# Gate and up projections of four feed-forward blocks as seven block products, in three parts of columns

## The chip, the cores and the metric

One core of a Trainium2 chip runs the whole program once. The metric is the device time of that execution in microseconds (us). The matrix engine is called PE (its weight loads are shown apart, as PEld), the vector engine DVE, the scalar engine ACT, GpSimd POOL, and SP is the queue that issues the weight transfers. PSUM holds eight banks of [128, 512] float32; each bank is where PE writes. SBUF is the on-chip memory that the other operands lie in.

## The reference

Two transformer-like layers on 512 tokens of width 1024, all in float32. There are four feed-forward blocks, two in each layer, all of one shape: the input is normalized, multiplied by a [1024, 5632] matrix, split into a gate and an up half of 2816 columns, and `silu(gate) * up` is multiplied by a [2816, 1024] matrix.

```
def _rmsnorm(x, g):
    y = xf * lax.rsqrt(jnp.mean(xf * xf, axis=-1, keepdims=True) + EPS)
    return (y * g.astype(jnp.float32)).astype(x.dtype)

def _swiglu(x, w_in, w_out):
    gate, up = jnp.split(x @ w_in, 2, axis=-1)
    return (jax.nn.silu(gate) * up) @ w_out

# first layer
x = x + 0.5 * _swiglu(_rmsnorm(x, n1_g[l]), ffn1_w_in[l], ffn1_w_out[l])
...  # two attention mixers, gated and added
x = x + 0.5 * _swiglu(_rmsnorm(x, n3_g[l]), ffn2_w_in[l], ffn2_w_out[l])
return _rmsnorm(x, nf_g)
...  # second layer: feed-forward, stick-breaking attention, feed-forward
```

## The kernel before, in words

The residual stream is kept transposed: eight tiles `x[k]` of [128 features, 512 tokens]. A matrix product in float32 is made of three products of float32r pairs: an operand is split into a high part (a copy with rounding, on ACT) and a low part (operand minus high part, on DVE), and `mm3` (lines 178 to 181) adds high*high, high*low and low*high in a bank. Every matmul has a [128, 128] piece of weights, loaded for it, and 512 tokens that move.

`plan` lists all weights in the order of their use, in chunks of up to [128, 1024]. `load_ahead` issues their transfers on SP, `split_ahead` splits them into `wh` (ACT, L156) and `wl` (DVE, L157), four chunks ahead of their use, and `weight` hands them out.

`ffn` (line 265) takes the 22 column blocks one after the other: a block is 128 gate columns and 128 up columns, 8 pieces of 128 features each, 48 matmuls. The gate is scaled by the tokens' norm `rs` (L274, DVE), goes through silu (L275, ACT), is multiplied with the up bank (L276, DVE) and split (L174 on ACT, L175 on DVE) into `hid`. The output projection then takes each of the eight output tiles with all 22 pieces of `hid` (66 matmuls), scales (L295) and adds to `x[m]` (L296), and `done(m)` starts what follows from `x[m]`. The norm's scale comes from squares (`Norm.add`: ACT squares, DVE adds), one matmul with ones (`total`, L232) and `rsqrt` (two ACT steps, three DVE steps). It is applied after the products, so PE needn't wait for it; the first `ffn` asks for it after its second column block (`at=1`).

PE, ACT and SP work in the order in which the program is written. On DVE and POOL a scheduler sets the order when the program is built. Each engine takes its instructions strictly in that order.

## Time and profile before

| what | value |
|---|---|
| runs | 2180.39, 2181.23, 2183.92 us (median 2181.23) |
| span of the profiled execution | 2182.6 us, 1.4 above the median |
| PE busy | 2153.3 us, 99% of the span, 9782 matmuls |
| PE weight loads busy | 1765.2 us, 81% |
| DVE busy | 1123.7 us, 51% |
| ACT busy | 883.0 us, 40% |
| POOL busy | 64.6 us, 3% |

A matmul's busy time runs from its start to its modelled end, and the next one starts before that end. So a busy PE is read by the distance from start to start and not by the sum of durations. DVE and ACT overlap their instructions a little in the same way. A row of the timeline or of the groups has the program's line, what was written and read, and the shape; `<-` at the end names who ended the idle time before it.

### The profile page before, as it was taken

Reading aid. Unit: us, or ns where it says so; the run is one execution under the profiler, and the core shown is the slowest. Engines: PE = TensorE matmul, PEld = TensorE weight load, DVE = VectorE, ACT = ScalarE, POOL = GpSimd, SP = SyncE. Lnnn points to the kernel's source line nnn. Section 1 sums busy time; section 2 is a strip of 40 time slices with the busy share of each in tenths; the row PEclk is TensorE's granted clock in tenths of the full one; section 3 lists DMA queues with packets and bytes.
Section 4 is the critical chain, followed back from the end, with each engine's and each line's share of the span. In section 5 each row is a group of like instructions: output and inputs, shape, how many; then the busy total and the mean of one; then the engine's idle time right before and its main releaser. Section 6 shows DMA issues by size and latency. Waiting matters only on the chain.

```text
span 2182.6 us, 24716 instructions
## 1 busy us (share of the span) xinstructions
PE 2153.3 (99%) x9782; PEld 1765.2 (81%) x9782; DVE 1123.7 (51%) x1659; ACT 883.0 (40%) x1415; POOL 64.6 (3%) x167
## 2 busy tenths in 40 slices
PE   8999999999999999999999999999999989999999
PEld 6888888887888788888888888888777768888887
DVE  6444334799843744444446444344687756444332
ACT  5222222376766442223233222223577665222211
POOL 0000000000000100000000000000011110000000
PEclk9999999999999999999999999999999999999999
DMA  4322233222211332222332222333111103222331
GB/s 163 111 97 98 82 105 119 89 87 73 70 48 49 117 104 97 97 96 81 105 104 91 99 98 94 92 96 97 58 44 44 49 19 107 97 97 97 97 120 53
DMA packets 57268, 193.42 MB, mean 89 GB/s; under 512 B 6784, under 2 KB 6784, under 8 KB 57152
## 3 DMA queue, kind: packets, MB, share of 16 engines
q1 hardware_dynamic: 55296, 188.28, 26.3%
q0 software_dynamic: 640, 2.10, 0.3%
q10 hardware_dynamic: 1216, 1.47, 0.2%
q8 instruction: 76, 1.25, 0.2%
q14 instruction: 40, 0.33, 0.0%
HBM read 189.07 MB, written 2.10 MB: 88 GB/s over the span
## 4 chain that ended last, share of the span: by engine, by line
PE 84%; issue 10%; DVE 4%; ACT 2%; DMA 0%; POOL 0%; SPq 0%; DVEq 0%; POOLq 0%
PE ps L179 25%; PE ps L180 25%; PE ps L181 25%; PE ps L803 2%; PE ps L869 1%; PE ps L848 1%; PE ps L732 1%; PE ps L734 1%; PE ps L733 1%; DVE wl L157 1%; PE ps L761 1%; PE ps L844 1%; PE ps L416 0%; PE ps L415 0%; DVE sl L498 0%
## 5 line engine op out<-in xcount | busy, mean ns | idle before, releaser
L179 PE MATMUL ps<-sl,wh 128*128 128x512 f32 x2704 | 1070.4, 396 | 11.5 <-ACT sl L246 6.6
L180 PE MATMUL ps<-sl,wh 128*128 128x512 f32 x2704 | 1055.7, 390 | 1.8 <-DVE sl L175 1.0
L181 PE MATMUL ps<-sl,wl 128*128 128x512 f32 x2704 | 1056.0, 391 | 0.0
L179 PEld LDWEIGHTS ps<-sl,wh 128*128 128x128 f32 x2704 | 509.7, 188 | 121.4 <-issue 7.0
L180 PEld LDWEIGHTS ps<-sl,wh 128*128 128x128 f32 x2704 | 509.6, 188 | 109.3 <-issue 3.4
L181 PEld LDWEIGHTS ps<-sl,wl 128*128 128x128 f32 x2704 | 509.1, 188 | 107.1 <-DVE wl L157 0.4
L157 DVE TENSOR_TENSOR wl<-wraw,wh 128x1024 fp32r<-128x1024 f32 (+3 forms) x368 | 434.8, 1183 | 289.5 <-ACT wh L156 289.0
L156 ACT ACTIVATE wh<-wraw 128x1024 fp32r<-128x1024 f32 (+3 forms) x368 | 372.9, 1015 | 520.6 <-issue 237.9
L174 ACT ACTIVATE sl<-sl 128x512 fp32r<-128x512 f32 x113 | 71.4, 632 | 394.9 <-DVE sl L276 384.0
L276 DVE TENSOR_TENSOR sl<-ps,sl 128x512 f32<-128x512 f32 x88 | 60.9, 692 | 267.2 <-PE ps L181 260.8
L274 DVE TENSOR_TENSOR sl<-ps,sl 128x512 f32<-128x512 f32 x88 | 60.8, 691 | 138.7 <-PE ps L181 138.6
L175 DVE TENSOR_TENSOR sl<-sl 128x512 fp32r<-128x512 f32 x113 | 79.9, 707 | 79.1 <-ACT sl L174 78.6
L227 ACT ACTIVATE sl<-x 128x512 f32<-128x512 f32 x42 | 25.8, 629 | 124.4 <-DVE x L296 97.7
L295 DVE SCALAR_TENSOR_TENSOR sl<-ps,sl 128x512 f32<-128x512 f32 x32 | 22.1, 691 | 80.0 <-PE ps L181 80.0
L275 ACT ACTIVATE sl<-sl 128x512 f32<-128x512 f32 x88 | 54.2, 616 | 12.2 <-DVE sl L274 12.2
L517 ACT ACTIVATE sl<-sl,mx 128x128 f32<-128x128 f32 (+3 forms) x64 | 35.9, 560 | 47.2 <-DVE mx L516 45.9
L823 POOL TENSOR_SCALAR_AFFINE_SELECT sl<-sl 128x128 f32<-128x128 f32 x64 | 23.1, 373 | 941.7 <-ACT sl L814 832.9
L594 PE MATMUL ps<-sl 128*128 128x256 f32 (+2 forms) x176 | 43.3, 327 | 1.3 <-DVE mx L516 1.3
L228 DVE TENSOR_TENSOR sl<-sl 128x512 f32<-128x512 f32 x49 | 33.3, 691 | 20.9 <-ACT sl L227 20.4
L524 ACT ACTIVATE sl<-sl,sm 128x128 f32<-128x128 f32 (+3 forms) x64 | 35.8, 559 | 15.8 <-DVE sm L523 7.3
L869 PE MATMUL ps<-sl 128*128 128x512 f32 (+3 forms) x128 | 38.7, 446 | 3.0 <-POOL sl L859 3.0
L817 DVE SCALAR_TENSOR_TENSOR sl<-ps,sl 128x512 f32<-128x512 f32 (+1 forms) x48 | 28.7, 597 | 24.2 <-ACT sl L815 23.8
(124 smaller groups left out, 1448.3 us busy)
## 6 DMA issues: line engine op xcount, KB each, us to landing
wraw<-in_f_in_dram SPq DMA_DIRECT2D x176, 512.0 KB
wraw<-in_f_out_dram SPq DMA_DIRECT2D x64, 512.0 KB
wraw<-in_mix_t_dram SPq DMA_DIRECT2D x34, 512.0 KB
wraw<-in_f_out_dram SPq DMA_DIRECT2D x32, 384.0 KB
wraw<-in_sb_qk_dram SPq DMA_DIRECT2D x16, 512.0 KB
wraw<-in_br_dram SPq DMA_DIRECT2D x16, 256.0 KB
wraw<-in_w_out_dram SPq DMA_DIRECT2D x8, 512.0 KB
wraw<-in_sb_v_dram SPq DMA_DIRECT2D x8, 512.0 KB
```

Source lines behind the costliest of these rows:

```text
L156: act.activation(wh[:, :n], raw[:, :n], AF.Copy)
L157: dve.tensor_tensor(wl[:, :n], raw[:, :n], wh[:, :n].bitcast(F32), op=OP.subtract)
L174: act.activation(h, x, AF.Copy)
L175: dve.tensor_tensor(l, x, h.bitcast(F32), op=OP.subtract)
L179: pe.matmul(ps, wh, xh, start=start, stop=False)
L180: pe.matmul(ps, wh, xl, start=False, stop=False)
L181: pe.matmul(ps, wl, xh, start=False, stop=stop)
L274: dve.tensor_tensor(g, pg, rs, op=OP.mult)
L275: act.activation(g, g, AF.Silu)
L276: dve.tensor_tensor(g, pu, g, op=OP.mult)
L803: pe.matmul(pz[b][:, c:c + w], k[hr, sb * P:(sb + 1) * P], q[hr, sb * P:], start=True, stop=True)
L869: pe.matmul(po[:, sb * P:], v[sb][n // 4][:, (n % 4) * P:(n % 4 + 1) * P], lb[b][:, c:c + w], start=sb == 0, stop=sb == 3)
```

## The change

In all four feed-forward blocks the gate and up projections of a column block are computed together as a 2 x 2 block product by Strassen's scheme in Winograd's form: weights in four [512 features, 128 columns] quarters, activations in four [512 features, 256 tokens] quarters, seven products P1 to P7 instead of eight. A product is 4 pieces x 3 = 12 matmuls with 256 moving tokens. The sums and differences before and after are made by the other engines:

- Weights, for each block (`piece`): POOL makes a sum (L190) and a difference (L191), DVE two differences (L196, L198), all [128, 512]. Then three [128, 1024] tiles and one [128, 512] tile are split on ACT and DVE (L180, L181, L173, L174). The tile of sums `wsum` has one buffer.
- Activations, once for a feed-forward block (`Combos`): for each pair of `x` tiles four [128, 256] differences, half on DVE and half on POOL, and splits of all.
- Results, for each block: four [128, 256] copies from PSUM on ACT (L398, L402, L409, L425), additions on DVE (L366, L418, L419, L421) and one on POOL (L426). Product 3 of a block comes after products 1 and 7 of the next one, so that its bank's copy (L425) can be made meanwhile.

The 22 blocks are taken in three parts of 7, 7 and 8; after each part the output projection runs over that part's `hid` and is added to `x[m]`, on POOL (L440) in the first two. The additions of squares go to POOL but for the last one (L276). The scale of the norm is now asked for in the first block. Slots go from 66 to 58, raw weight buffers from 2 to 4; a few long-lived tiles move to a pool for each stage. The transfers of a block are two of 512 KB as before.

```diff
-    for n in range(2 * NF):
-        plan.append((a["f1_in"][n], 1024))
...
+    def ffn_chunks(w_in, w_out):
+        f = 0
+        for nf_ in PARTS:
+            for n in range(f, f + nf_):
+                for j in range(4):
+                    plan.append((w_in[n], (n, j)))
+            for m in range(KD):
+                plan.append((w_out[m][:, f * P:(f + nf_) * P], nf_ * P))
+            f += nf_
...
+    def quarter(src):
+        wh = stage["pool"].tile([P, 512], F32R, name="w4h", tag="w4h", bufs=2)
+        wl = stage["pool"].tile([P, 512], F32R, name="w4l", tag="w4l", bufs=2)
+        act.activation(wh, src, AF.Copy)
+        dve.tensor_tensor(wl, src, wh.bitcast(F32), op=OP.subtract)
+        return wh, wl
...
+    def piece(r, j):
+        gate, up = r["gate"], r["up"]
+        if j == 0:
+            r["s"] = stage["pool"].tile([P, 1024], F32, name="wsum", tag="wsum", bufs=1)
+            pool.tensor_tensor(r["s"][:, :512], up[:, :512], up[:, 512:], op=OP.add)
+            pool.tensor_tensor(up[:, :512], gate[:, :512], up[:, :512], op=OP.subtract)
+            return std_halves(gate, 1024)
+        if j == 1:
+            return std_halves(up, 1024)
+        if j == 2:
+            dve.tensor_tensor(r["s"][:, 512:], r["s"][:, :512], gate[:, :512], op=OP.subtract)
+            return std_halves(r["s"], 1024)
+        dve.tensor_tensor(gate[:, 512:], gate[:, 512:], r["s"][:, 512:], op=OP.subtract)
+        return quarter(gate[:, 512:])
...
-                dve.tensor_tensor(self.acc, self.acc, sq, op=OP.add)
+                (dve if last else pool).tensor_tensor(self.acc, self.acc, sq, op=OP.add)
...
+        def pair(self, b1, b2):
+            lo, hi = slice(0, 256), slice(256, 512)
+            ta, tb = sl(), sl()
+            dve.tensor_tensor(ta[:, lo], b1[:, hi], b1[:, lo], op=OP.subtract)
+            pool.tensor_tensor(ta[:, hi], b2[:, hi], b1[:, hi], op=OP.subtract)
+            dve.tensor_tensor(tb[:, lo], b2[:, hi], ta[:, lo], op=OP.subtract)
+            pool.tensor_tensor(tb[:, hi], b2[:, lo], tb[:, lo], op=OP.subtract)
+            b11 = sl(F32R)
+            act.activation(b11[:, lo], b1[:, lo], AF.Copy)
+            dve.tensor_tensor(b11[:, hi], b1[:, lo], b11[:, lo].bitcast(F32), op=OP.subtract)
+            ah, al = split(ta)
+            bh, bl = split(b2)
+            ch, cl = split(tb)
...
+        def product(n, ps, w, c0, ks, first, last=True):
+            for k in ks:
+                c = slice(c0 + k * P, c0 + (k + 1) * P)
+                h, l = xs.sets[k][n]
+                st_, en = first and k == 0, last and k == 3
+                pe.matmul(ps[:, :256], w[0][:, c], h, start=st_, stop=False, skip_group_check=True)
+                pe.matmul(ps[:, :256], w[0][:, c], l, start=False, stop=False, skip_group_check=True)
+                pe.matmul(ps[:, :256], w[1][:, c], h, start=False, stop=en, skip_group_check=True)
...
+                    product(1, f["b"], u1, 0, allk, True)
+                    act.copy(f["s"][:, lo], f["b"][:, :256])
+                    split_ahead()
+                    u2 = weight(src, (n, 1))
+                    product(7, f["c"], u2, 0, allk, True)
+                    act.copy(f["s"][:, hi], f["c"][:, :256])
+                    split_ahead()
+                if old is not None:
+                    product(3, old["b"], old["u4"], 0, allk, False)
+                    gate_ready(old)
+                u3 = weight(src, (n, 2))
+                product(6, f["b"], u3, 512, allk, False)
+                act.copy(f["u"][:, lo], f["b"][:, :256])
+                if old is not None:
+                    finish(old)
+                split_ahead()
+                if n != 0:
+                    f["a"] = bank()
+                    product(2, f["a"], u1, 512, allk, True)
+                if n == 0:
+                    rs = rstd()
+                dve.tensor_tensor(f["g"][:, lo], f["a"][:, :256], f["s"][:, lo], op=OP.add)
+                dve.tensor_tensor(f["g"][:, lo], f["g"][:, lo], rs[:, lo], op=OP.mult)
+                product(4, f["c"], u2, 512, allk, False)
+                dve.tensor_tensor(f["up"][:, lo], f["c"][:, :256], f["u"][:, lo], op=OP.add)
+                if old is not None:
+                    hid.append(split(old["g"]))
+                product(5, f["b"], u3, 0, allk, False)
+                act.copy(f["u"][:, hi], f["b"][:, :256])
+                pool.tensor_tensor(f["up"][:, hi], f["u"][:, hi], f["s"][:, hi], op=OP.add)
+                f["u4"] = weight(src, (n, 3))
+                split_ahead()
+                old = f
...
+                (dve if final else pool).tensor_tensor(x[m], x[m], t, op=OP.add)
...
-NSLOT = 66
-RAW_BUFS = 2
+NSLOT = 58
+RAW_BUFS = 4
+LOAD_AHEAD = 8
+PARTS = (7, 7, 8)
```

The order of the instructions at three places.

On DVE, one column block in the middle of the first feed-forward. Before, it is the split of the two weight chunks (`wl`), the scaled gate, the product with up, and the split of `hid`:

```order
L157 TENSOR_TENSOR wl<-wraw,wh 128x1024
L276 TENSOR_TENSOR sl<-ps,sl 128x512
L175 TENSOR_TENSOR sl<-sl 128x512
L157 TENSOR_TENSOR wl<-wraw,wh 128x1024
L274 TENSOR_TENSOR sl<-ps,sl 128x512
```

Of the change, the block after next, the next and the last one stand mixed: L196, L198 and L181 belong to weights of later blocks, L366, L371 and L222 to the block before:

```order
L196 TENSOR_TENSOR wsum<-wsum,wraw 128x512
L174 TENSOR_TENSOR w4l<-wraw,w4h 128x512
L181 TENSOR_TENSOR wl<-wraw,wh 128x1024
L198 TENSOR_TENSOR wraw<-wraw,wsum 128x512
L181 TENSOR_TENSOR wl<-wraw,wh 128x1024
L366 TENSOR_TENSOR sl<-ps,sl 128x256
L371 TENSOR_TENSOR sl<-sl 128x512
L418 TENSOR_TENSOR sl<-ps,sl 128x256
L419 TENSOR_TENSOR sl<-sl 128x256
L181 TENSOR_TENSOR wl<-wsum,wh 128x1024
L421 TENSOR_TENSOR sl<-ps,sl 128x256
L222 TENSOR_TENSOR sl<-sl 128x512
```

Five instructions a block became twelve; `ps` among the sources is PSUM, and the others read SBUF alone.

On POOL, between the program's start and the mixer. Before, nothing of the first feed-forward stands there, only fills:

```order
L318 MEMSET adm_186 128x128
L319 MEMSET adm_186 64x64
L337 MEMSET sl_2503 128x512
L337 MEMSET sl_2504 128x512
L337 MEMSET sl_2505 128x512
```

Of the change, in the middle of its first part (numbers tell the buffers apart; two blocks of weights, and the addition of an earlier block's result):

```order
L426 TENSOR_TENSOR sl_389<-sl_387,sl_386 128x256
L190 TENSOR_TENSOR wsum_538<-wraw_391 128x512
L191 TENSOR_TENSOR wraw_391<-wraw_390,wraw_391 128x512
L190 TENSOR_TENSOR wsum_669<-wraw_522 128x512
L191 TENSOR_TENSOR wraw_522<-wraw_521,wraw_522 128x512
L426 TENSOR_TENSOR sl_520<-sl_518,sl_517 128x256
```

Three POOL instructions a block are new, and the weights' two stand ahead of the result's one.

On ACT, behind the last square of the first norm (L227 before, L275 now). Before, weights and the norm's logarithm follow:

```order
L227 ACTIVATE sl<-x_79 128x512
L156 ACTIVATE wh<-wraw 128x1024 x4
L237 ACT_TABLE_LOAD
L208 ACTIVATE sl<-ps,epst 128x512
L209 ACTIVATE sl<-sl 128x512
```

Of the change, the first copies from PSUM (L391, L393) stand there:

```order
L275 ACTIVATE sl<-x_79 128x512
L391 COPY sl<-ps 128x256
L393 COPY sl<-ps 128x256
L180 ACTIVATE wh<-wraw 128x1024 x2
L409 COPY sl<-ps 128x256
L180 ACTIVATE wh<-wsum 128x1024
L285 ACT_TABLE_LOAD
L256 ACTIVATE sl<-ps,epst 128x512
L257 ACTIVATE sl<-sl 128x512
```

PE's product 6, which adds to the bank that L391 reads, now waits behind all of ACT's work on `x`.

## Rows read from the trace of the kernel before

**Rows 1.** Page: busy us of PE; granted clock in 40 slices.

```profile
PE 2153.3 (99%) x9782; PEld 1765.2 (81%) x9782; DVE 1123.7 (51%) x1659; ACT 883.0 (40%) x1415; POOL 64.6 (3%) x167
...
PEclk9999999999999999999999999999999999999999
```

**Rows 2.** Timeline (start us, length us, what): PE inside one column block.

```profile
100.22 0.39 PE L179 MATMUL ps<-sl,wh 128*128 128x512 f32 x1
...
102.94 0.39 PE L179 MATMUL ps<-sl,wh 128*128 128x512 f32 x1
```

**Rows 3.** Groups by shape (count, busy us, mean ns, idle): 256-column matmuls.

```profile
L848 PE MATMUL ps<-sl,ones_r 128*128 128x256 f32 x64 | 12.9, 282 | 0.0
```

**Rows 4.** Timeline of PE at such a place: two of them in one row.

```profile
1571.18 0.40 PE L848 MATMUL ps<-sl,ones_r 128*128 128x256 f32 x2
```

**Rows 5.** Timeline of the weight loads there: four of them in one row.

```profile
1571.30 0.53 PEld L844 LDWEIGHTS ps<-sl,cmat 128*128 128x128 f32 x4
```

**Rows 6.** Timeline of DVE in one column block (in brackets: idle before).

```profile
111.40 0.69 DVE L175 TENSOR_TENSOR sl<-sl 128x512 fp32r<-128x512 f32 x1 [0.70 <-ACT sl L174]
...
115.38 0.69 DVE L274 TENSOR_TENSOR sl<-ps,sl 128x512 f32<-128x512 f32 x1 [1.81 <-PE ps L181]
...
120.89 0.69 DVE L276 TENSOR_TENSOR sl<-ps,sl 128x512 f32<-128x512 f32 x1 [3.37 <-PE ps L181]
```

**Rows 7.** Groups by shape on DVE.

```profile
L157 DVE TENSOR_TENSOR wl<-wraw,wh 128x1024 fp32r<-128x1024 f32 x314 | 384.6, 1226 | 220.1 <-ACT wh L156 219.8
...
L830 DVE TENSOR_TENSOR sl<-sl 128x256 fp32r<-128x256 f32 x16 | 6.8, 425 | 1.2
...
L712 DVE SCALAR_TENSOR_TENSOR x<-x,gains,sl 128x512 f32<-128x512 f32 x8 | 5.8, 742 | 0.0
```

**Rows 8.** Timeline of DVE beside the POOL products at L664, mixer gates.

```profile
705.83 1.76 DVE L666 TENSOR_TENSOR sl<-sl 128x512 f32<-128x512 f32 x1 [0.97 <-POOL sl L664]
...
709.22 0.68 DVE L665 TENSOR_TENSOR sl<-ps,sl 128x512 f32<-128x512 f32 x1
709.82 0.68 DVE L175 TENSOR_TENSOR sl<-sl 128x512 fp32r<-128x512 f32 x1
710.42 1.77 DVE L157 TENSOR_TENSOR wl<-wraw,wh 128x512 fp32r<-128x512 f32 x1
...
715.31 0.68 DVE L665 TENSOR_TENSOR sl<-ps,sl 128x512 f32<-128x512 f32 x1
...
720.53 1.21 DVE L157 TENSOR_TENSOR wl<-wraw,wh 128x1024 fp32r<-128x1024 f32 x1
721.66 1.78 DVE L175 TENSOR_TENSOR sl<-sl 128x512 fp32r<-128x512 f32 x1
```

**Rows 9.** Timeline of POOL in the same stretch.

```profile
709.90 1.74 POOL L664 TENSOR_TENSOR sl<-sl 128x512 f32<-128x512 f32 x1 [1.15 <-ACT sl L656]
715.10 1.44 POOL L664 TENSOR_TENSOR sl<-sl 128x512 f32<-128x512 f32 x1 [3.46 <-ACT sl L656]
...
721.03 1.87 POOL L664 TENSOR_TENSOR sl<-sl 128x512 f32<-128x512 f32 x1 [1.58 <-ACT sl L656]
723.54 1.29 POOL L664 TENSOR_TENSOR sl<-sl 128x512 f32<-128x512 f32 x1 [0.65 <-ACT sl L656]
```

**Rows 10.** Groups by shape on ACT.

```profile
L156 ACT ACTIVATE wh<-wraw 128x1024 fp32r<-128x1024 f32 x314 | 330.3, 1053 | 434.8 <-issue 205.4 <-PE ps L180 180.3 <-DMA wraw<-in_f_in_dram 14.7
L174 ACT ACTIVATE sl<-sl 128x512 fp32r<-128x512 f32 x113 | 71.4, 632 | 394.9 <-DVE sl L276 384.0 <-DVE sl L666 10.3
...
L533 ACT COPY sl<-ps 128x256 f32<-128x256 f32 x16 | 5.8, 361 | 0.2
```

**Rows 11.** Timeline of ACT at the start of the kernel.

```profile
5.83 5.59 ACT L246 ACTIVATE sl<-x,gains 128x512 fp32r<-128x512 f32 x8 [0.29 <-DMA x<-in_x_dram]
...
19.62 3.74 ACT L227 ACTIVATE sl<-x 128x512 f32<-128x512 f32 x7
```

**Rows 12.** Chain that ended last: the first feed-forward's sum of squares.

```profile
32.87 0.86 PE ps L232 x2
```

More of the change, by code (lines that the diff above doesn't have):

```diff
@@ L136, in block_kernel, with stage_pool @@
         plan.append((a["sb_o"][m], 1024))
-    for n in range(2 * NF):
-        plan.append((a["f4_in"][n], 1024))
-    out_chunks(a["f4_out"])
+    ffn_chunks(a["f4_in"], a["f4_out"])
     raws, ready, taken = [], [], [0]
-    def load_ahead(most=SPLIT_AHEAD + RAW_BUFS):
+    stage = {}
+    def stage_pool(name):
+        if "ctx" in stage:
+            stage["ctx"].__exit__(None, None, None)
+        stage["ctx"] = tc.tile_pool(name=name, bufs=1)
+        stage["pool"] = stage["ctx"].__enter__()
@@ new lines, in quarter, with std_halves @@
+    def quarter(src):
[4 more added lines that the diff above has]
+        return wh, wl
+    def std_halves(raw, n):
+        wh = wpool.tile([P, 1024], F32R, name="wh", tag="wh", bufs=SPLIT_AHEAD + 1)
+        wl = wpool.tile([P, 1024], F32R, name="wl", tag="wl", bufs=SPLIT_AHEAD + 1)
+        act.activation(wh[:, :n], raw[:, :n], AF.Copy)
+        dve.tensor_tensor(wl[:, :n], raw[:, :n], wh[:, :n].bitcast(F32), op=OP.subtract)
+        return wh, wl
@@ L153, in split_ahead @@
             raw, n = raws[c], plan[c][1]
-            wh = wpool.tile([P, 1024], F32R, name="wh", tag="wh", bufs=SPLIT_AHEAD + 1)
-            wl = wpool.tile([P, 1024], F32R, name="wl", tag="wl", bufs=SPLIT_AHEAD + 1)
-            act.activation(wh[:, :n], raw[:, :n], AF.Copy)
-            dve.tensor_tensor(wl[:, :n], raw[:, :n], wh[:, :n].bitcast(F32), op=OP.subtract)
-            ready.append((wh, wl))
+            ready.append(std_halves(raw, n) if isinstance(n, int) else piece(raw, n[1]))
             raws[c] = None
@@ L219, in __init__, with add @@
             self.acc = None
[L221 removed]
+        def add(self, t, scale=1.0, last=True):
             if self.acc is None:
@@ L263, in run, with __init__, add @@
             pass
[L265 to L297 removed]
+    class Combos:
+        def __init__(self):
+            self.rows = []
+            self.sets = []
+        def add(self, t, g):
+            xg = sl()
+            act.activation(xg, t, AF.Copy, scale=g)
+            self.rows.append(xg)
+            if len(self.rows) == 2:
+                self.pair(*self.rows)
+                self.rows = []
+        def pair(self, b1, b2):
[11 more added lines that the diff above has]
+            ch, cl = split(tb)
+            self.sets.append({
+                1: (b11[:, lo], b11[:, hi]), 2: (bh[:, lo], bl[:, lo]), 3: (bh[:, hi], bl[:, hi]),
+                4: (ch[:, hi], cl[:, hi]), 5: (ah[:, lo], al[:, lo]), 6: (ch[:, lo], cl[:, lo]),
+                7: (ah[:, hi], al[:, hi])})
@@ L399, in stack_a @@
         T[n] = f(t, LOW), f(t, HIGH)
-    vab = [sl() for _ in range(4)]
+    vab = [st() for _ in range(4)]
     vb = consts.tile([P, 4, 136], F32, name="vb")
@@ L740, in finish @@
             for b in range(4):
-                v[b][half] = sl()
+                v[b][half] = st() if half == 0 else sl()
                 dve.tensor_scalar(v[b][half], pv[b], rcol2[:, b:b + 1], None, op0=OP.mult)
@@ L921, in block_kernel @@
         dve.tensor_tensor(x[m], ps, x[m], op=OP.add)
-        norm.add(x[m])
-        xs.append(scaled_split(x[m], gain(G_F2, m)))
+        xs.add(x[m], gain(G_F2, m))
+        norm.add(x[m], last=m == KD - 1)
     def done4(m):
```

142 lines of the change are left out of this document (86 added, 56 removed).

## The prediction

> **What bounds the kernel now.** I read the page's busy shares first. PE is busy for 2153 of 2182.6 us, at a granted clock that stays in its top tenth [rows 1]. Inside the feed-forward blocks it never waits: in the timeline twelve matmuls of 512 columns start within 2.72 us, 0.2267 us apart [rows 2]. A column block of 48 matmuls therefore takes 10.88 us, and the 88 blocks of the four feed-forwards take 957 us. DVE has time in such a block: it sits idle for 1.8 and for 3.4 us before its two steps on PE's banks [rows 6]. ACT and POOL have more. So PE is the bound, and a change that takes columns from PE cuts into it; the question is which engine takes its place.
>
> **PE's own part.** A block becomes 7 x 12 = 84 matmuls of 256 columns. The columns fall by an eighth; the matmuls go from 48 to 84, each with its own weight load. Half of 0.2267 is 0.113 us. The one place with such matmuls back to back has two in 0.40 us, and one of them takes 0.282, so the second starts 0.12 behind the first [rows 3, 4]. Four loads take 0.53 us where one takes 0.19, so they can follow every 0.113 us [rows 5]. I take 0.1165: 9.8 us a block (9.5 to 10.1). If PE stayed the bound, 88 blocks would give 88 x 1.1 = 95 us (70 to 120) back.
>
> **DVE and POOL in a block.** DVE's steps start 0.60 us apart for 512 columns and 1.13 for 1024 [rows 8]; a 256-column one takes 0.425 in all [rows 7], about 0.34 from start to start. The new order has three of 1024 (L181), five of 512 and four of 256: 3.4 + 3.0 + 1.4 = 7.8 us. That alone would fit into 9.8. POOL has two additions of 512 columns, 1.29 us each when nothing is in the way [rows 9], and one of 256. No row shows that one; it lies between half and the whole of 1.29, and I take 0.7. The Trainium skill's "GPSIMD Engine Reference" (section "Elementwise — side-by-side cycle accounting") gives about 2.6 cycles an element and 4497 ns for 2048; an estimate from that page for 256 is also 0.7 us.
>
> The two engines can't run side by side here. Where DVE read two SBUF operands while a POOL product ran, it took 1.76 to 1.78 us in place of 0.68, and POOL took 1.74 and 1.87 in place of 1.29 [rows 8, 9]: each waited for the other to end. A DVE step that read PSUM and SBUF, at 715.31 us within the POOL step of 715.10, took its 0.68 [rows 8, 9]. Of DVE's 7.8 us here, 6.7 read SBUF alone. With POOL's 3.3 that is 10.0 us for one block, where PE wants 9.8.
>
> The order makes it worse. `wsum` has one buffer, so POOL's sum for a later block starts only when DVE has ended its split (the third L181). From that end, t = 0: L421 runs beside POOL's sum, which ends at 1.3; L222 to 1.9; POOL's difference L191 to 3.1; L196 to 3.7; POOL's L426 to 4.4; L174 to 5.0; L181 to 6.1; L198 to 6.7; L181 to 7.9; L366 to 8.2. L371 waits for silu on ACT, which waits for L366: 0.7 us with nothing to do (silu on 512 columns takes what ACT's copy takes, 0.63 [rows 10], and two handovers). Then L371 to 9.5, L418 to 9.9, L419 (it reads L418's result) to 10.4, and the next L181 to 11.5. **DVE's cycle is 11.5 us a block, more than the 10.88 of today.**
>
> PE isn't held by that at once, since weights are split a block ahead, and the output projection, where DVE has little to do, refills this lead ahead of each of the twelve parts. Counted from a part's first product, PE alone would start block j (from 0) at 8.4 + 9.8 (j - 1), since the first has no product 3 of a block before. DVE opens its cycle at 18.7 in block 1 (block 0 without L222 and without contention in its first half) and 11.5 later in each further one: 30.2, 41.7, 53.2. On ACT the copy of a block's last bank (L425) stands behind silu and split of the block before, 10.8 behind that opening: L371 at 9.5, the split (0.63 [rows 10]) behind a weight tile, the copy (0.36 [rows 10]). So block 5's product 3 can start at 53.2 + 10.8 = 64.0 in place of 60.2. Its 1.4 and four more products (5.6) end at 71.0; the last copy behind its queue takes 0.8 and the last product 3 another 1.4: a part of seven ends at 73.3 us. Seven blocks today take 76.2. A part of eight ends at 84.8 against 87.1. The output projection behind it starts on six finished pieces of `hid` (18 matmuls, 4.1 us), which hide the last piece's way over DVE and ACT (4.3 us) but for 0.2. So a part brings 2.8 or 2.2 us, where PE alone would bring 7.2 or 8.3 (it would end at 69.0 and 78.8).
>
> **Starts.** Today the first norm's sum comes at 32.9 to 33.7 us, after two blocks [rows 12]; five more end at 88.1. In the change ACT must make all activation splits before PE's product 6, because the first copies from PSUM stand behind them. Today's eight scalings take 5.6 us [rows 11]. A pair of tiles now needs two scalings (1.4), a 256 copy (0.3), three splits (1.6) and waits of about 1.0 for DVE and POOL, which make its differences one after the other: 4.3 us, so four pairs end at about 24. Two weight tiles and the quarter (2.6) and eight squares at 0.52 us each, start to start [rows 11], follow: 31. PE has by then done 36 short matmuls, does product 6 to 32.9 and stands before the norm's matmul. That waits for seven additions on POOL, with `wsum` and its difference for the next block between them: from 27.6 us nine steps of 1.25 and four DVE splits that contend, about 43. Behind it L196, which needs POOL's next sum, stands ahead of the norm's first DVE step. DVE's cycle starts at 57.2 in place of 18.7, and the first part ends at 57.2 + 54.6 = 111.8 against 88.1: **+24 us** (18 to 30).
>
> In feed-forwards 2 and 4 the same L196 and three norm steps of 0.73 delay DVE's cycle by 6 us: the first part ends at -2.8 + 6 = +3. Feed-forward 3 has besides ten more norm steps, among them eight of 0.742 (L712 [rows 7]): +10. And in the last output projection of feed-forward 2, DVE and POOL must make the splits of `x`, twelve additions of squares (15 us of POOL) and the next weights: about 31 + 21 us in 43.6 us of PE's matmuls. That lag of some 10 us (5 to 13) reaches PE at feed-forward 3. First part there: -2.8 + 6 + 10 + 10 = **+23**.
>
> The rest costs nothing. Output projections keep their number of matmuls. Bytes are the same, two of 512 KB a block, and four raw buffers give each transfer a block's time. POOL's additions to `x` (1.3 us) lie beside 4.8 us of PE for each output tile; without that cover they would be 10 us a part. The mixers are as before but for fewer slots.
>
> **The sum.** Eight later parts: 4 x (-2.8) + 4 x (-2.2) = -20. First parts: 24 + 3 + 23 + 3 = +53. Against the span of 2182.6 us this gives 2216; the median of the runs lies 1.4 lower: **2214 us, 1.5% slower**.
>
> **Rivals.**
> 1. *PE stays the bound in the parts.* It ends on the other side. Place: the twelve part loops. The lead of 5.7 us lasts for a part of seven when DVE's cycle is 10.4 us or less, so it is decided by whether 1.1 of POOL's 3.3 us falls where DVE waits for silu or reads PSUM. For it: four such steps a block, and a DVE that is already late waits for nothing else. Against it: POOL's sum becomes free just when DVE has SBUF steps queued. Price: later parts 4 x (-7.2) + 4 x (-8.3) = -62, starts 19 - 1 + 15 - 1 = +32, together 2182.6 - 30 - 1.4, 2151 us. Chance 0.25.
> 2. *POOL is hidden wholly* (DVE's cycle under 9.8): the starts shrink too, to about 10 + 0 + 3 + 0 against first parts of today: 2130 us at most, 2120 with PE at 9.6 a block. Chance 0.08.
> 3. *The lead at a part's start isn't there* (first weights late, or slots that come free late): 11.5 us from the first block on, 88 x 0.6 = +55, with starts of 24 + 6 + 26 + 6 = 62: 2298 us; with half the lead lost, 2256. Chance 0.13.
> 4. *The change doesn't halve a matmul:* at 0.1295 us for 256 columns a block costs 10.88 on PE and nothing is won. The 0.12 of [rows 4] speaks against it. Together with ends of the others near zero, 2177 to 2186: chance 0.06.
>
> **How the numbers follow.** Forecast (slower, up to 2250): 0.48. Faster by over 0.2% (4.4 us, about what a measurement here can tell): rivals 1 and 2 = 0.33. Same: 0.06. Slower: 0.48 + 0.13 = 0.61. Both signs have weight, so the range takes in rival 1 and half of rival 3: 2130 to 2258 leaves out 0.08 below and about 0.1 above. The forecast's own range, from its bounds (starts 40 to 70, parts -35 to 0), is 2185 to 2250.
>
> **What would show it.** In the new profile: DVE steps of 1024 columns in the part loops that take 1.8 to 2.5 us where 1.23 is undisturbed; blocks about 11.5 us apart in a part's second half and 9.8 in its first; PE waiting there for ACT (L425's copy) and DVE (`wl`); PE idle between 33 and 43 us with POOL's L276 as releaser; POOL busy for over 400 us. It is wrong if DVE's 1024-column steps stay near 1.23 us, or if the blocks in a part's second half are 10 us apart.

## The result and the profile after

The changed kernel takes 2238.0 us (median of four runs, 2237.4 to 2238.8) against 2181.4 us before: 1.026 times as long (95% interval 1.024 to 1.027), 57 us slower. The prediction was slower, 2214 us.

The page of the changed kernel, its busy shares and the granted clock:

```profile
PE 2108.1 (94%) x12950; PEld 1868.1 (84%) x12950; DVE 1718.3 (77%) x2372; ACT 1151.0 (51%) x2007; POOL 613.7 (27%) x558
...
PEclk9999999999999999999998999999999999999999
```

Against [rows 1], PE has lost its 99%: it is busy for 94% of a longer span. What it waits for stands in the view of the waits (what waited, for whom, us in all, times, longest):

```profile
PE ps L360 <- ACT sl L425: 45.5, 46, 4.8
PE ps L360 <- ACT sl L338: 28.0, 6, 11.0
PE ps L361 <- DVE sl L339: 14.1, 8, 5.6
PE ps L280 <- POOL sl L276: 10.3, 1, 10.3
```

The first line is the blocks: product 3 waits for the copy of a bank on ACT. The other three are starts: the splits of the activations (L338, L339) and the sum of squares (L276). ACT, 51% busy in all, comes late to that copy because it is released late: before silu (L370) it sits idle for 3.71 us until DVE has ended L366 (timeline of one block in the middle of the first part: start us, length us, what, idle before in brackets):

```profile
92.52 0.63 ACT L370 ACTIVATE sl<-sl 128x512 f32<-128x512 f32 x1 [3.71 <-DVE sl L366]
93.06 1.04 ACT L180 ACTIVATE wh<-wsum 128x1024 fp32r<-128x1024 f32 x1
94.00 0.61 ACT L221 ACTIVATE sl<-sl 128x512 fp32r<-128x512 f32 x1
94.52 0.35 ACT L425 COPY sl<-ps 128x256 f32<-128x256 f32 x1
```

So the chain is read on DVE and POOL, in the same block. DVE:

```profile
84.31 0.42 DVE L421 TENSOR_TENSOR sl<-ps,sl 128x256 f32<-128x256 f32 x1
84.64 1.67 DVE L222 TENSOR_TENSOR sl<-sl 128x512 fp32r<-128x512 f32 x1
86.23 1.77 DVE L196 TENSOR_TENSOR wsum<-wsum,wraw 128x512 f32<-128x512 f32 x1
87.93 1.23 DVE L174 TENSOR_TENSOR w4l<-wraw,w4h 128x512 fp32r<-128x512 f32 x1
89.08 1.21 DVE L181 TENSOR_TENSOR wl<-wraw,wh 128x1024 fp32r<-128x1024 f32 x1
...
92.07 0.42 DVE L366 TENSOR_TENSOR sl<-ps,sl 128x256 f32<-128x256 f32 x1
93.25 0.69 DVE L371 TENSOR_TENSOR sl<-sl 128x512 f32<-128x512 f32 x1 [0.77 <-ACT sl L370]
...
95.79 0.42 DVE L421 TENSOR_TENSOR sl<-ps,sl 128x256 f32<-128x256 f32 x1
```

POOL in the same stretch:

```profile
84.47 1.29 POOL L190 TENSOR_TENSOR wsum<-wraw 128x512 f32<-128x512 f32 x1 [7.35 <-DVE wl L181]
85.84 1.62 POOL L191 TENSOR_TENSOR wraw<-wraw 128x512 f32<-128x512 f32 x1
87.42 1.19 POOL L426 TENSOR_TENSOR sl<-sl 128x256 f32<-128x256 f32 x1
```

Read the two side by side. L222 is issued at 84.64, while L190 runs, and ends 0.55 us after L190's end at 85.76: 1.67 us for a step that takes 0.68 alone. L191 then waits for L222, L196 for L191, L426 for L196, L174 for L426: each ends 0.5 to 1.2 us after the one before it. DVE loses 1.0 + 1.1 + 0.55 = 2.6 us in these three steps. L421, which reads PSUM, overlaps the same L190 for 0.26 us (84.47 to 84.73); it takes its 0.42 and L190 its 1.29. From one L421 to the next is 11.48 us: the 11.5 of the prediction, row for row in its order. The Trainium skill's "SBUF — State Buffer" (section "Who interferes with whom") says that a DVE instruction with two SBUF inputs contends with a GpSimd instruction that reads SBUF, over a shared port pair that it calls "an exclusive lock", and that one with at most one SBUF input (outside DVE's 2-port modes) does not contend; both halves of that agree with these rows.

PE inside a block (where it has just waited for L425, and then goes on):

```profile
94.93 0.39 PE L360 MATMUL ps<-sl,w4h 128*128 128x256 f32 x1 [0.96 <-ACT sl L425]
95.15 0.28 PE L361 MATMUL ps<-sl,w4h 128*128 128x256 f32 x1
95.27 0.28 PE L362 MATMUL ps<-sl,w4l 128*128 128x256 f32 x1
95.39 0.28 PE L360 MATMUL ps<-sl,w4h 128*128 128x256 f32 x1
```

Undisturbed they start 0.12 apart (the median of all product matmuls): a block is 84 x 0.12 = 10.08 us where the 48 of before took 10.88 [rows 2]. So PE gained 0.8 us a block, 70 us in all, and the time went up by 57.

Where it went is seen by parts, from the start of a part's first product to the end of its last (its start and one distance from start to start). The parts of before are the same blocks, cut at 7, 14 and 22; for feed-forward 1 both are counted from the start of the trace, for the others from the first matmul of the feed-forward or part:

| stretch | before, us | after, us | difference |
|---|---|---|---|
| feed-forward 1, first part (end) | 88.0 | 115.9 | +27.9 |
| feed-forward 2, first part | 77.0 | 82.3 | +5.3 |
| feed-forward 3, first part | 77.9 | 102.1 | +24.1 |
| feed-forward 4, first part | 77.0 | 89.7 | +12.6 |
| four later parts of seven | 76.2 each | 73.7 each | -9.7 |
| four later parts of eight | 87.0 each | 85.2 each | -7.2 |
| sum | | | +53.0 |

The spans differ by 2236.3 - 2182.6 = 53.7 us; the other 0.7 lies in output projections (38.1, 38.1 and 43.5 us by count of matmuls) and mixers. So the later parts gain 17 us, a third of the 48 that their 60 blocks at 0.8 promise, and the first parts lose four times that.

The times differ by 57, 3 us more than the spans: the median lies 1.7 us above the profile's span in the changed kernel, and 1.2 below it in the kernel before. In what follows the first part of feed-forward 1 is counted from its own first product too; so counted it takes 106.9 us in the changed kernel.

### The profile page after: what moved, and what is told of

Its sections match the earlier page's. It is cut to its first block, busy times and chain, and to the rows that moved or that the text cites. A ratio compares the mean times of both kernels' runs of the same rounds, so it can differ in the third digit from the quotient of the medians.

```text
span 2236.3 us, 33026 instructions
## 1 busy us (share of the span) xinstructions
PE 2108.1 (94%) x12950; PEld 1868.1 (84%) x12950; DVE 1718.3 (77%) x2372; ACT 1151.0 (51%) x2007; POOL 613.7 (27%) x558
## 4 chain that ended last, share of the span: by engine, by line
PE 42%; DVE 26%; issue 20%; ACT 7%; POOL 5%; DMA 0%; POOLq 0%; DVEq 0%; ACTq 0%
DVE wl L181 7%; PE ps L226 7%; PE ps L227 7%; PE ps L228 7%; PE ps L360 4%; PE ps L362 4%; PE ps L361 4%; DVE sl L222 3%; DVE wsum L196 3%; DVE w4l L174 2%; ACT wh L180 2%; POOL x L440 2%; POOL wsum L190 1%; PE ps L952 1%; PE ps L1018 1%
## 5 line engine op out<-in xcount | busy, mean ns | idle before, releaser
L360 PE MATMUL ps<-sl,wh 128*128 128x256 f32 x2112 | 605.4, 287 | 34.0 <-ACT sl L338 28.0
L361 PE MATMUL ps<-sl,wh 128*128 128x256 f32 x2112 | 603.5, 286 | 14.9 <-DVE sl L339 14.1
L362 PE MATMUL ps<-sl,wl 128*128 128x256 f32 x2112 | 601.5, 285 | 0.5 <-DVE wl L181 0.5
L226 PE MATMUL ps<-sl,wh 128*128 128x512 f32 x1296 | 519.3, 401 | 4.6 <-ACT sl L221 4.6
L181 DVE TENSOR_TENSOR wl<-wraw,wh 128x1024 fp32r<-128x1024 f32 (+3 forms) x368 | 464.0, 1266 | 74.7 <-ACT wh L180 71.4
L180 ACT ACTIVATE wh<-wraw 128x1024 fp32r<-128x1024 f32 (+3 forms) x368 | 374.6, 1020 | 273.1 <-PE ps L227 126.6
L227 PE MATMUL ps<-sl,wh 128*128 128x512 f32 x1296 | 506.7, 391 | 1.0 <-DVE sl L222 1.0
L228 PE MATMUL ps<-sl,wl 128*128 128x512 f32 x1296 | 506.5, 391 | 0.0
L360 PEld LDWEIGHTS ps<-sl,wh 128*128 128x128 f32 x2112 | 409.2, 194 | 38.2 <-ACT sl L338 29.1
L361 PEld LDWEIGHTS ps<-sl,wh 128*128 128x128 f32 x2112 | 409.4, 194 | 19.3 <-DVE sl L339 16.1
L362 PEld LDWEIGHTS ps<-sl,wl 128*128 128x128 f32 x2112 | 409.4, 194 | 0.8 <-DVE wl L181 0.8
L226 PEld LDWEIGHTS ps<-sl,wh 128*128 128x128 f32 x1296 | 244.0, 188 | 58.4 <-ACT sl L221 6.4
L227 PEld LDWEIGHTS ps<-sl,wh 128*128 128x128 f32 x1296 | 244.2, 188 | 52.3 <-DVE sl L222 3.9
L228 PEld LDWEIGHTS ps<-sl,wl 128*128 128x128 f32 x1296 | 243.8, 188 | 52.2 <-DVE wl L181 0.4
L190 POOL TENSOR_TENSOR wsum<-wraw 128x512 f32<-128x512 f32 x88 | 121.3, 1378 | 477.5 <-DVE wl L181 421.7
L222 DVE TENSOR_TENSOR sl<-sl 128x512 fp32r<-128x512 f32 x161 | 174.7, 1098 | 29.0 <-ACT sl L221 28.3
L370 ACT ACTIVATE sl<-sl 128x512 f32<-128x512 f32 x88 | 55.6, 632 | 232.7 <-DVE sl L366 232.6
L196 DVE TENSOR_TENSOR wsum<-wsum,wraw 128x512 f32<-128x512 f32 x88 | 128.5, 1460 | 45.5 <-POOL wsum L190 45.5
L426 POOL TENSOR_TENSOR sl<-sl 128x256 f32<-128x256 f32 x88 | 109.0, 1238 | 188.0 <-ACT sl L425 188.0
L191 POOL TENSOR_TENSOR wraw<-wraw 128x512 f32<-128x512 f32 x88 | 148.5, 1687 | 5.8
L360 PE MATMUL ps<-sl,w4h 128*128 128x256 f32 x352 | 104.5, 297 | 45.5 <-ACT sl L425 45.5
```

Source lines behind the costliest of these rows:

```text
L180: act.activation(wh[:, :n], raw[:, :n], AF.Copy)
L181: dve.tensor_tensor(wl[:, :n], raw[:, :n], wh[:, :n].bitcast(F32), op=OP.subtract)
L190: pool.tensor_tensor(r["s"][:, :512], up[:, :512], up[:, 512:], op=OP.add)
L191: pool.tensor_tensor(up[:, :512], gate[:, :512], up[:, :512], op=OP.subtract)
L196: dve.tensor_tensor(r["s"][:, 512:], r["s"][:, :512], gate[:, :512], op=OP.subtract)
L222: dve.tensor_tensor(l, x, h.bitcast(F32), op=OP.subtract)
```

## The experiments

**Theory 1, turns.** DVE steps that read only SBUF and POOL's additions wait for each other; DVE's cycle of 11.5 us bounds the blocks, and POOL's work in turns with DVE makes the starts long. **Theory 2** had DVE's own steps and its waits for ACT as the cause, with POOL's work nearly free.

**Weights' sums on DVE.** This gives DVE more to do and takes away most turns.

```diff
-            pool.tensor_tensor(r["s"][:, :512], up[:, :512], up[:, 512:], op=OP.add)
-            pool.tensor_tensor(up[:, :512], gate[:, :512], up[:, :512], op=OP.subtract)
+            dve.tensor_tensor(r["s"][:, :512], up[:, :512], up[:, 512:], op=OP.add)
+            dve.tensor_tensor(up[:, :512], gate[:, :512], up[:, :512], op=OP.subtract)
```

> The weights' sum and difference (L190, L191) go from POOL to DVE: DVE gets 1.2 us more a block, POOL keeps only L426 there. Theory 1, turns (a DVE step that reads only SBUF and a POOL addition wait for each other; DVE loses 2.6 us a block to that): DVE's cycle falls from 11.5 to about 10.6 us, later parts of seven from 73.7 to 71 to 72 us, of eight from 85.2 to 81 to 82, first parts some 5 us each shorter, in all about 2192 us (2180 to 2210). Theory 2, DVE's own steps and its waits for ACT make the cycle and POOL's work beside them costs it little: the cycle grows by the 1.2 to 12.7 us, parts grow by 5 to 7 us, in all about 2305 us.

Measured: 2185.8 us, 52 us faster than the changed kernel for 1.2 us more DVE work in each block; against the kernel before 1.0018 (1.0008 to 1.0027). Later parts take 71.1 and 81.2 us, which is PE's own 588 x 0.12 = 70.6 and 672 x 0.12 = 80.6; the first parts 101.9, 77.0, 93.4 and 83.0. PE's waits for L425 fell from 45.5 to 8.9 us:

```profile
PE ps L360 <- ACT sl L425: 8.9, 13, 3.4
PE ps L280 <- POOL sl L276: 7.2, 1, 7.2
```

Theory 2 would have had 2305. Moving two 0.6 us steps from POOL to DVE shortened DVE's block, since on POOL they had cost it 2.1 us of waiting (L222 and L196 above).

**POOL's addition three times.** The opposite test gives POOL more to do: DVE, ACT and PE keep their instructions.

```diff
                 pool.tensor_tensor(f["up"][:, hi], f["u"][:, hi], f["s"][:, hi], op=OP.add)
+                pool.tensor_tensor(f["up"][:, hi], f["u"][:, hi], f["s"][:, hi], op=OP.add)
+                pool.tensor_tensor(f["up"][:, hi], f["u"][:, hi], f["s"][:, hi], op=OP.add)
```

> POOL's addition L426 (256 columns) is done three times in a row, same values; DVE, ACT and PE have the same instructions as in the changed kernel. POOL is idle for 7.35 us of a block there. Theory 1, turns: two more POOL steps of 0.73 us, each of which holds up a DVE step: DVE's cycle goes from 11.5 to about 12.8 us, later parts of seven from 73.7 to about 79, of eight from 85.2 to about 91.7, in all about 2310 us (2290 to 2330). Theory 2 (POOL's work beside DVE costs little): within 3 us of 2238.

Measured: 2319.0 us, 81 more, from work that POOL had 7.35 us of idle time a block for. Later parts take 79.2 and 91.9. The two added steps on POOL and DVE's steps beside them:

```profile
91.12 1.07 POOL L427 TENSOR_TENSOR sl<-sl 128x256 f32<-128x256 f32 x1
92.27 1.60 POOL L428 TENSOR_TENSOR sl<-sl 128x256 f32<-128x256 f32 x1
```

```profile
91.52 1.76 DVE L181 TENSOR_TENSOR wl<-wraw,wh 128x1024 fp32r<-128x1024 f32 x1
93.31 1.11 DVE L198 TENSOR_TENSOR wraw<-wraw,wsum 128x512 f32<-128x512 f32 x1
...
96.65 0.69 DVE L371 TENSOR_TENSOR sl<-sl 128x512 f32<-128x512 f32 x1 [0.77 <-ACT sl L370]
```

L181 goes from 1.21 to 1.76, L198 from 0.69 to 1.11; from one L371 to the next is 12.45 us (the one before starts at 84.20). The two added steps write what L371 reads, and neither L181 nor L198 needs their result: these wait for POOL's engine and not for its data. With the first run this settles it between the two theories.

**The same work in the kernel before.** Does a turn always cost time? Here POOL gets three additions of 512 columns in each block of the kernel before, into a tile that nobody reads.

```diff
             dve.tensor_tensor(g, pu, g, op=OP.mult)
+            for _ in range(3):
+                pool.tensor_tensor(scr, g, g, op=OP.add)
             hid.append(split(g))
...
+    scr = consts.tile([P, S], F32, name="scr")
```

> The kernel before with POOL work it doesn't need: in each of the 88 column blocks three additions of 512 columns behind the product of silu and up, whose result nobody reads; about 3.9 us of POOL a block, more than the changed kernel has there. DVE's own steps in such a block are 2 x 1.13 + 3 x 0.60 = 4.1 us of 10.88. Theory 1, turns that cost only where DVE is late: DVE's steps beside POOL take 1.7 to 1.8 us in place of 0.68 and up to 2.3 in place of 1.23, DVE stays under 8 us a block, PE doesn't wait and the time stays within 0.3% of the kernel before (2175 to 2188 us). Rival, POOL's additions slow PE's or ACT's work too, or DVE's delays reach PE anyway: 1.5 us a block or more, above 2310 us.

Measured: 2181.9 us, 1.000 of the kernel before (0.999 to 1.001). The turns are there, in the groups by shape (count, busy us, mean ns, idle):

```profile
L157 DVE TENSOR_TENSOR wl<-wraw,wh 128x1024 fp32r<-128x1024 f32 x314 | 448.7, 1430 | 200.8 <-ACT wh L156 199.8
L175 DVE TENSOR_TENSOR sl<-sl 128x512 fp32r<-128x512 f32 x113 | 106.2, 939 | 82.6 <-ACT sl L174 82.2
L276 DVE TENSOR_TENSOR sl<-ps,sl 128x512 f32<-128x512 f32 x88 | 60.9, 691 | 262.4 <-PE ps L181 256.4 <-ACT sl L275 6.0
```

The mean of L157 was 1226 in [rows 7] and is 1430; 89 us of DVE time, and none of it reaches PE, because DVE sits idle before its two PSUM steps [rows 6]. L276, which reads PSUM, stays at 0.69. Here, then, a turn costs time only where DVE is the one that is late.

**The product of silu moved back.** In the block above DVE waits 0.77 us for ACT. Here L371 stands behind the gate steps L418 and L419.

```diff
             act.activation(g, g, AF.Silu)
-            dve.tensor_tensor(g, f["up"], g, op=OP.mult)
+        def times(f):
+            tc.keep_in_program_order(dve.tensor_tensor(f["g"], f["up"], f["g"], op=OP.mult))
...
                 dve.tensor_tensor(f["g"][:, lo], f["g"][:, lo], rs[:, lo], op=OP.mult)
+                if old is not None:
+                    times(old)
                 product(4, f["c"], u2, 512, allk, False)
```

> The product of silu and up (L371) is moved on DVE behind the two gate steps L418 and L419, so that ACT's silu is done when DVE comes to it; nothing else changes. If DVE's queue is the cycle (theories 1 and 2 alike): its idle 0.77 us a block goes, the cycle falls from 11.5 to about 10.7, later parts of seven to 71 to 72 us, of eight to 81.5 to 82.5, in all about 2200 us (2195 to 2215). Rival, the cycle is a loop through POOL and the one wsum buffer in which DVE's idle time is only slack: the wait turns up elsewhere, within 4 us of 2238.

Measured: 2214.2 us, 24 less. DVE's rows (its L366, L420, L421, L373 are L366, L418, L419, L371 of the changed kernel):

```profile
70.57 0.42 DVE L366 TENSOR_TENSOR sl<-ps,sl 128x256 f32<-128x256 f32 x1
...
71.70 0.68 DVE L373 TENSOR_TENSOR sl<-sl 128x512 f32<-128x512 f32 x1
72.64 1.23 DVE L181 TENSOR_TENSOR wl<-wsum,wh 128x1024 fp32r<-128x1024 f32 x1 [0.26 <-ACT wh L180]
...
81.55 0.42 DVE L366 TENSOR_TENSOR sl<-ps,sl 128x256 f32<-128x256 f32 x1
```

From L366 to L366 is 10.98 us, where 10.7 was expected: a third of the wait came back before L181, which now comes too early for ACT's split of the sums. Later parts take 71.7 and 82.6 us. DVE's queue is the bound, as in both theories, and the rival falls: two thirds of the idle time were won, so it was more than slack in a loop through the one `wsum` buffer. A second `wsum` buffer wasn't tried.

**The starts: squares on DVE.**

```diff
-                (dve if last else pool).tensor_tensor(self.acc, self.acc, sq, op=OP.add)
+                dve.tensor_tensor(self.acc, self.acc, sq, op=OP.add)
```

> All additions of squares (L276) are on DVE, as in the kernel before; POOL keeps the weights' and results' additions. Theory 1: what makes the first parts long is POOL's chain of additions that take turns with DVE (six in 10.9 us at the start of feed-forward 1, with PE idle from 34.4 to 45.0). On DVE they take 0.6 each: PE waits there until about 37, first parts 8 us shorter in feed-forward 1, 8 in 3, 4 in 4, 2 in 2, in all about 2216 us (2208 to 2225). Rival, DVE's queue at the starts is what is late whoever adds: seven more DVE steps make each first part 2 to 4 us longer, about 2250 us.

Measured: 2223.5 us, 14.6 less in place of 22. The first parts fell by 6.8, 1.9, 2.9 and 4.6 us (8, 2, 8 and 4 were expected); all later parts stayed at 73.7 and 85.2. In the changed kernel POOL and PE at the start of feed-forward 1 (whose seven additions are all on POOL, the last one too) read

```profile
34.03 10.89 POOL L276 TENSOR_TENSOR sl<-sl 128x512 f32<-128x512 f32 x6
```

```profile
44.98 2.07 PE L280 MATMUL ps<-sl,cmat 128*128 128x512 f32 x2 [10.34 <-POOL sl L276]
```

and with the squares on DVE PE's wait there is

```profile
PE ps L280 <- DVE sl L276: 3.7, 1, 3.7
```

So the direction holds and the rival (DVE has no room at the starts) falls, but feed-forward 3 kept 5 us that were put down to the squares. How much of the gain is turns isn't separated: without them six additions of 1.29 would still take 7.7 of the 10.89 us on POOL, and the run takes away POOL's own pace together with the turns.

**The starts: the norm asked for later**, with all of POOL's work left as it is.

```diff
+                if n == 1:
+                    rs = rstd()
+                    dve.tensor_tensor(old["g"][:, lo], old["g"][:, lo], rs[:, lo], op=OP.mult)
                 if old is not None:
                     product(3, old["b"], old["u4"], 0, allk, False)
...
-                if n == 0:
-                    rs = rstd()
...
-                dve.tensor_tensor(f["g"][:, lo], f["g"][:, lo], rs[:, lo], op=OP.mult)
+                if n != 0:
+                    dve.tensor_tensor(f["g"][:, lo], f["g"][:, lo], rs[:, lo], op=OP.mult)
```

> The changed kernel with one edit: the norm is asked for in the second block in place of the first; all of POOL's work stays. PE's 10.3 us wait at 34.4 to 45.0 goes by 5.6. If that wait is itself the loss of the first part, 5 us less in feed-forward 1, 3 to 5 in 3: about 2228 us. If the queues of DVE and POOL behind it are the loss (theory 1: PE would wait as long a little later), within 3 us of 2238.

Measured: 2229.4 us, 8.6 less. The first part of feed-forward 1 went from 106.9 to 101.5 us, 5.4 of the 5.6 us of products that PE can do meanwhile; feed-forward 3's fell by only 1.2. In feed-forward 1, PE's wait for the sum was itself a loss; the expectation that the queues behind it would eat it up, which was theory 1's, fell here.

**Both moves together.** The weights' sums and the squares on DVE, the edits of the two kernels that had them singly, together.

```diff
-            pool.tensor_tensor(r["s"][:, :512], up[:, :512], up[:, 512:], op=OP.add)
-            pool.tensor_tensor(up[:, :512], gate[:, :512], up[:, :512], op=OP.subtract)
+            dve.tensor_tensor(r["s"][:, :512], up[:, :512], up[:, 512:], op=OP.add)
+            dve.tensor_tensor(up[:, :512], gate[:, :512], up[:, :512], op=OP.subtract)
...
-                (dve if last else pool).tensor_tensor(self.acc, self.acc, sq, op=OP.add)
+                dve.tensor_tensor(self.acc, self.acc, sq, op=OP.add)
```

> Only the weights' sums (L190, L191) and the squares (L276) are on DVE; POOL keeps the results' addition, the activation differences and the additions to x. If the two moves act on different waits (blocks and starts) their gains add: 2185.8 - 14.6 = about 2171 us (2166 to 2178). If both act on the same DVE queue at the starts, the second brings under half of it: 2179 to 2186 us.

Measured: 2170.9 us, 0.995 of the kernel before (0.993 to 0.996). Gains add to within 0.3 us. The first parts are 98.6, 73.4, 88.8 and 78.9.

**All of POOL's additions on DVE**: besides the weights' sums and the squares, the differences of the activations (L334, L336), the results (L426) and `x` (L440) too.

```diff
-            pool.tensor_tensor(ta[:, hi], b2[:, hi], b1[:, hi], op=OP.subtract)
+            dve.tensor_tensor(ta[:, hi], b2[:, hi], b1[:, hi], op=OP.subtract)
...
-                pool.tensor_tensor(f["up"][:, hi], f["u"][:, hi], f["s"][:, hi], op=OP.add)
+                dve.tensor_tensor(f["up"][:, hi], f["u"][:, hi], f["s"][:, hi], op=OP.add)
...
-                (dve if final else pool).tensor_tensor(x[m], x[m], t, op=OP.add)
+                dve.tensor_tensor(x[m], x[m], t, op=OP.add)
```

> Nothing that takes turns is left on POOL: weights' sums (L190, L191), results' addition (L426), squares (L276), activation differences (L334, L336) and the additions to x of the first two parts (L440) are all on DVE. Theory 1: DVE's cycle is about 9.4 us of steps and some 0.5 of waits, still under PE's 10.08, so later parts stay at PE's 71 and 81 us; first parts fall by 8, 1, 6 and 4 us against the kernel with the weights' sums alone on DVE (2185.8): about 2166 us (2155 to 2178), faster than before. Rival: DVE has no room at the starts, the moved steps make first parts longer again: 2190 to 2200 us.

Measured: 2166.9 us, 0.993 of the kernel before (0.991 to 0.994). Later parts stay at 71.1 and 81.1; first parts 97.2, 72.4, 87.6 and 79.1. The rest on POOL was worth 4 us.

**The late norm on top of that**, in all four feed-forwards.

```diff
+                if n == 1:
+                    rs = rstd()
+                    dve.tensor_tensor(old["g"][:, lo], old["g"][:, lo], rs[:, lo], op=OP.mult)
                 if old is not None:
                     product(3, old["b"], old["u4"], 0, allk, False)
...
-                if n == 0:
-                    rs = rstd()
```

> As the kernel with all on DVE, and the norm is asked for in the second block, ahead of its product 3, in place of the first: PE has four more products (5.6 us) to do before it comes to the norm's matmul, and the first block's gate is scaled later. If PE's wait for the sum of squares is what the first parts still lose, 3 to 5 us less in feed-forward 1 and 3 and 1 to 2 in the others than with all on DVE: about 2157 us. Rival, DVE's queue decides when the first blocks end: the wait moves behind the norm, within 3 us of the kernel with all on DVE.

Measured: 2162.7 us, 4.2 less (9 were expected). Feed-forward 1's first part went from 97.2 to 91.3, feed-forward 3's from 87.6 up to 90.3: there the norm brings seventeen DVE steps, and that part got longer when they came a block later; what they meet there was not taken apart.

**The late norm in feed-forward 1 alone.**

```diff
-    def ffn(xs, rstd, w_in, w_out, done):
+    def ffn(xs, rstd, w_in, w_out, done, at=0, extra=None):
...
+                if n == 1 and at == 1:
+                    rs = rstd()
...
-                if n == 0:
+                if n == 0 and at == 0:
                     rs = rstd()
...
-    ffn(xs, norm.rstd, a["f1_in"], a["f1_out"], done1)
+    ffn(xs, norm.rstd, a["f1_in"], a["f1_out"], done1, at=1)
```

> All additions on DVE as before, and the late norm in feed-forward 1 alone. In the kernel with the late norm in all four, the first part of feed-forward 1 was 91.3 us (97.2 without it) and that of feed-forward 3 was 90.3 (87.6 without it). If these two are independent, 3's is back at 87.6 and 1's stays at 91.3: about 2160 us (2157 to 2163). Rival, run to run and scheduler differences of this size: no change against 2162.7.

Measured: 2158.9 us, 0.989 of the kernel before (0.988 to 0.991). This is the fastest version that was run, 79 us under the changed kernel. First parts 90.7, 72.4, 87.6 and 78.9. Two groups of its DVE by shape, and PE's waits:

```profile
L222 DVE TENSOR_TENSOR sl<-sl 128x512 fp32r<-128x512 f32 x161 | 110.4, 697 | 25.9 <-ACT sl L221 25.4
...
L196 DVE TENSOR_TENSOR wsum<-wsum,wraw 128x512 f32<-128x512 f32 x88 | 60.2, 684 | 0.0
```

```profile
PE ps L360 <- ACT sl L338: 17.1, 5, 9.0
PE ps L360 <- ACT sl L429: 11.0, 15, 3.3
```

The same two groups in the changed kernel:

```profile
L222 DVE TENSOR_TENSOR sl<-sl 128x512 fp32r<-128x512 f32 x161 | 174.7, 1098 | 29.0 <-ACT sl L221 28.3
L196 DVE TENSOR_TENSOR wsum<-wsum,wraw 128x512 f32<-128x512 f32 x88 | 128.5, 1460 | 45.5 <-POOL wsum L190 45.5
```

Their means fell from 1098 and 1460 ns to 697 and 684, so neither waits for turns now. Of the 44 us that the later parts of this version gain on the kernel before, its starts still eat 19: against before the first parts are 11.7 us longer (counted from the start of the trace), 4.7 shorter, 9.7 longer and 1.9 longer.

**The scaling of `x` in feed-forward 3 put off** until its first part is done, on top of the version just shown.

```diff
     def ffn3_norm():
-        r2 = rstd_pair()
-        for m in range(KD):
-            dve.scalar_tensor_tensor(x[m], x[m], gain(G_NF, m), state["nf"], op0=OP.mult, op1=OP.mult)
-        return r2
+        return rstd_pair()
...
+            if part == 0 and extra is not None:
+                extra()
             for m in range(KD):
```

> As the kernel with the late norm in feed-forward 1 alone, and the eight scalings of x in feed-forward 3 (L712 in the kernel before, 0.742 us each on DVE, 5.9 us in all) come behind its first part, ahead of the output projection, in place of right behind the norm. If DVE's queue is what still makes that first part 87.6 us long (PE's own 588 matmuls of 0.12 take 70.6), it falls to 81.5 to 83.5 us, about 2155 us in all. Rival, the first part waits for the activations' differences and splits ahead of the norm, not for these steps: 87 us and within 1.5 us of the other kernel.

Measured: 2160.1 us, no better than the 2158.9. The first part of feed-forward 3 fell by 2.0 us to 85.6, not by 5, and the gain was given back later: the last output projection and the mixer behind it, from the end of the part of eight to feed-forward 4, take 367.8 us in place of 364.6. Why was not followed up, and what holds that first part at 86 us stays open.

## Why the prediction was right, and where it was off

*What takes PE's place.* Right, and shown: DVE in turns with POOL. The cycle was put at 11.5 us and is 11.48; the order of the waits is the one written down. The run with more POOL work and the one with less both moved as turns say, far from the rival.

*What a part brings.* Right: 73.3 and 84.8 us were forecast for later parts, 73.7 and 85.2 measured. The lead is seen in the starts of ACT's L425 in the second part, at 162.9, 172.9, 183.5, 195.0, 206.4 and 217.9 us: 10.0, 10.6, then 11.5 apart. Eight later parts were to bring 20 us and brought 17.

*PE's price.* 0.1165 was taken and 0.12 measured, 10.08 us a block in place of 9.8. It moved the forecast little (a part's end by some 0.2 us), since PE wasn't the bound, but it is why the kernels with all work on DVE stop at 71.1 and 81.1.

*What the profile should show.* One sign was named wrongly. DVE's steps of 1024 columns were to take 1.8 to 2.5 us; in a steady block they take 1.21 and it is L222, L196 and L174, of 512 columns, that wait, as the prediction's own list of times from t = 0 has it. The mean of all of them is 1.33 us, close to the undisturbed 1.23, which the prediction had put down as a sign that it is wrong; that sign did not fit the working behind it. The others came: PE waits for L425 (45.5 us), blocks 11.5 apart in a part's second half, PE idle from 34.4 to 45.0 at L276 (33 to 43 was said), POOL busy for 614 us.

*The starts.* This is the step whose size was off: +53 forecast, +70 measured, 17 of the 24 us by which 2214 missed. (Of the other 7, 3 are the later parts, 1 the projections and mixers, and 3 the step from span to median, 1.4 us down in the forecast and 1.7 up in the measurement.) Feed-forward 1 and 3 were near (+24 and +23 against +27.9 and +24.1), feed-forward 2 was +5.3 for +3. (For feed-forward 3 ten more norm steps were counted; there are fourteen more.) Feed-forward 4 was to be +3 and is +12.6. The prediction gave a lag of DVE and POOL in the stage ahead to feed-forward 3 alone. But feed-forward 4 comes out of a mixer's output projection that makes the same splits, squares and differences, and there DVE reads

```profile
1868.81 1.21 DVE L181 TENSOR_TENSOR wl<-wsum,wh 128x1024 fp32r<-128x1024 f32 x1
1869.94 1.75 DVE L174 TENSOR_TENSOR w4l<-wraw,w4h 128x512 fp32r<-128x512 f32 x1
1871.61 1.48 DVE L333 TENSOR_TENSOR sl<-sl 128x256 f32<-128x256 f32 x1
1873.01 1.21 DVE L196 TENSOR_TENSOR wsum<-wsum,wraw 128x512 f32<-128x512 f32 x1
1874.14 1.48 DVE L335 TENSOR_TENSOR sl<-sl 128x256 f32<-128x256 f32 x1
```

while PE waits for the last pair:

```profile
1876.01 0.58 PE L361 MATMUL ps<-sl,wh 128*128 128x256 f32 x1 [5.63 <-DVE sl L339]
```

Two weight steps stand in front of the pair's first difference (L333) and one in front of its second (L335). On POOL, L190, L334 and L191 run beside them:

```profile
1871.10 1.71 POOL L190 TENSOR_TENSOR wsum<-wraw 128x512 f32<-128x512 f32 x1
1872.77 0.90 POOL L334 TENSOR_TENSOR sl<-sl 128x256 f32<-128x256 f32 x1
1873.63 1.71 POOL L191 TENSOR_TENSOR wraw<-wraw 128x512 f32<-128x512 f32 x1
```

L174, L333, L196 and L335 take 0.68, 0.41, 0.68 and 0.42 alone, so the turns in these rows come to 3.7 us, most of PE's wait of 5.63. The kernel with the sums and the squares on DVE bears this out: its first part there is 78.9 us, 1.9 above before in place of 12.6. It takes POOL's slower additions away together with the turns, so the share of each in the 12.6 isn't shown. For feed-forward 1, 2 of the missing 4 us are POOL's chain, which ended at 44.9 and not 43; the rest was not taken apart.

*The rivals.* Rival 1 (PE stays the bound in the parts) lost in the changed kernel, and rival 2 (DVE's cycle under 9.8 us) falls by the 11.48. The condition of rival 1 was right: with two of POOL's three steps gone, the parts are at PE's time. Its price for the starts was too kind, though. With the parts at PE's 71 and 81 the run took 2185.8 and not 2151: the first parts lost 23.4 (feed-forward 1's ends at 111.4), 0, 15.5 and 6.0 us, 45 where 32 was written, and the later parts gained 44, not 62, at 0.12 a matmul. Rival 3 (no lead) is shown wrong by the 10.0 and 10.6, rival 4 by the 0.12.

*POOL's small addition.* 0.7 us was taken for 256 columns, between the bounds that the rows gave, and 0.73 measured. The second way to it doesn't come out at 0.7: an eighth of the 4497 ns that the prediction quotes from the Trainium skill's "GPSIMD Engine Reference" (section "Elementwise — side-by-side cycle accounting") is 0.56 us. The forecast doesn't rest on that.
